# List scheduler of a hybrid SSD and gated-DeltaNet layer: later assumed landings for scratch transfers in DRAM

## The chip, the cores and the metric

The kernel runs on one core of one Trainium2 chip. The metric is the time of one execution in microseconds of device time; the median of several executions is compared. One execution was taken by the hardware profiler, and every row below is from that one.

## The reference

The reference computes one layer of a diffusion backbone in float32: 512 latent tokens and 256 context tokens of width 1024. A conditioning vector gives shifts, scales and gates (adaLN); a projection `w_in` feeds two groups of heads, which run over the tokens forwards and backwards; then come an output projection, an MLP with squared ReLU and a last RMSNorm.

```python
p_lat = modulate(rmsnorm(x, norm1_g[l]), sh1, sc1) @ w_in[l]
p_ctx = modulate(rmsnorm(ctx, norm1_g[l]), sh1c, sc1c) @ w_in[l]
y_lat, y_ctx = token_mixers(p_lat, p_ctx, ...)   # conv, SiLU, SSD scan, gated delta rule
x = x + g1 * (y_lat @ w_out[l])
x = x + g2 * sq_relu_mlp(modulate(rmsnorm(x, norm2_g[l]), sh2, sc2), w_mlp1[l], w_mlp2[l])
...
return rmsnorm(x, final_g)
```

The gated delta rule (`gdn_scan`) needs, for each chunk, the solution of a triangular system with a unit diagonal. The kernel inverts these triangular matrices ahead of the scan.

## The kernel before, in words

Every large product is taken in three parts, since a float32 weight is split into a high part `wH` (ScalarE casts it) and a low part `wL` (GpSimd subtracts); so a projection is 8 blocks of the width times 3 matmuls. `pl_k3` is the accumulator of the fourth key projection over 512 latent tokens (24 matmuls of 128x512), `pc_k3` that over 256 context tokens (24 matmuls of 128x256). The letters are k, q, v, g (heads of the delta rule), x, z, B, C (SSD). The raw weight columns come into two buffers `st_...` that are used in turn: the load of `st_x3` must wait until `st_x2` has been split.

Work in order: the modulation and `h` (0 to 40 us of the span); the projections k, q, g, v, B, C; beside them four inversions b = 0 to 3 (`inverse`, two heads each); then the SSD (`ssd`, eight steps ct = 0 to 7) and four scans (`scan`, 24 dependent steps in all) with the projections x and z as filler; then the output projection in two halves (`wo0a`, `wo1a`), and the MLP (`m1p`, `m2a`).

An inversion (line 671 on, `inverse`) goes through DRAM three times, since blocks change partitions there:

- `At` goes out to `blkD` in four transfers of 32x12x32 elements (rows of 128 bytes) and comes back as `ND`, `YD`. VectorE eliminates inside 32x32 blocks (30 dependent steps, tiles `YD`, `TD`).
- `YD` and `ND` go to `invD`; six loads fill `X`, four `Yf`, four `Yb`, each 48 KB in rows of 128 bytes.
- TensorE joins the blocks in steps that depend on each other, with 32x32 and 64x64 matmuls: `z1` (from `X`), `x1` and `y1` (from `Yf`, `Yb`), `z2`, `y2`; ScalarE copies between them. `Yf` and `Yb` go to `invF`, from where a scan loads them as `Ys`.

The trace leaves numbers out: `z<-X,At` there is z1 and z2 of all inversions.

The order of instructions on each engine is not that of the code. `kernel` traces the program once, and `_plan` builds a graph of it (`_Graph`) and plays it through in a model of the five engines (`_Graph.run`): on each engine the instruction that is ready and has the smallest key goes next. The key is mainly the place in the traced program, less the length of the longest path to the end (`rank`). The order found is then forced on each engine (`_keep`). SP, the engine that issues nearly all DMAs, is one of the five, so DMAs are in an order too: one that waits holds up those behind it. In hardware nothing of the model's times remains, only the order.

What the model assumes of a transfer stands in `_cost` (the time in the shared queue, `gap`, and what passes after it until the landing, `d`) and in `run` (2000 ns more):

```python
gap = b / (380.0 if same else 400.0 if run >= 2048 else 320.0 if run >= 512 else 60.0 if src.startswith("in_") else 150.0)
total = b / (300.0 if src.startswith("in_") else 140.0) + 600.0
d = max(0.0, total - gap)
...
end, fr = queue + self.dur[k] + 2000.0, t + (370.0 if e == 4 else 150.0)
```

`run` in `_cost` is the length of a row in bytes, and a source whose name begins with `in_` is an input of the kernel; every other source counts as scratch: loads from DRAM scratch, stores to it, and the stores of the output. An instruction on TensorE that needs a transfer's data is not ready before `end`; until then the model puts other ready work there.

Of the kernel before, what the change touches and what calls it, by code (L numbers as in the profile page):

```python
# [1394 lines left out]
_WINDOW = 3413.4  # L1395
_SLACK = (0.0, 100.0, 100.0, 100.0, 0.0)
_LANES = 8
_MIX = 1.2e9
_STRETCH = 1.0


def _name(ap):
    return getattr(ap, "memref", None) or ""
# [9 lines left out]
class _Graph:  # L1413
    def __init__(self, nc, tc, traced, ordered):
# [22 lines left out]
        for k, i in enumerate(self.ins):  # L1437
            d, s = set(), set()
# [39 lines left out]
        for i in self.ins:  # L1478
            e = _ENG.index(str(i.engine).split(".")[1])
            self.eng.append(e)  # L1480
            self.dma.append(kind[i.name] == "InstDMACopy")
            self._cost(i, e, kind[i.name], psum)
        for m in range(n):
            deps[m].discard(m)
            self.need[m] = len(deps[m])
            for d in deps[m]:
                same = self.eng[d] == self.eng[m] and not (self.dma[d] and d in sync[m])
                self.succ[d].append((m, same, d in sync[m]))

    def _cost(self, i, e, kind, psum):  # L1490
        table, accum, lock, shape = 0, False, False, 0
        w = _width(i.outs[0])
        gap = None
        if kind == "InstDMACopy":
            src = _name(i.ins[0])
            b = 4
            for q in i.outs[0].ap:
                b *= q[1]
            run = 4 * min(i.ins[0].ap[-1][1], i.outs[0].ap[-1][1])
            same = any(q[0] == 0 and q[1] > 1 for q in i.ins[0].ap)  # L1500
            gap = b / (380.0 if same else 400.0 if run >= 2048 else 320.0 if run >= 512 else 60.0 if src.startswith("in_") else 150.0)
            total = b / (300.0 if src.startswith("in_") else 140.0) + 600.0
            d = max(0.0, total - gap)
        elif e == 0:
            shape = tuple(i.tile_size)
            full = str(i.ins[0].dtype).endswith("float32") and str(i.ins[1].dtype).endswith("float32")
            if i.is_transpose:
                gap = max(84.0, 20 + 0.7 * w)
            elif not full:
                gap = 15 + 0.415 * w  # L1510
            elif shape == (32, 32):
                gap = 34.0
            elif shape[1] < 128:
                gap = 5 + 1.7 * w
            else:
                gap = max(218.0, 5 + 1.7 * w)
            d = gap + 163.0
            shape = (shape, tuple(i.tile_position or ()), full and not i.is_transpose)
        else:
            sp = [a for a in i.ins if hasattr(a, "memref") and _width(a) > 1]  # L1520
            ps = any(_name(a) in psum for a in sp)
            two = len(sp) > 1
            if e == 1:
                lock = not ps and kind != "InstMemset"
                if kind == "InstTensorTensor":
                    d = 145 + 1.04 * w
                elif kind == "InstReciprocal":
                    d = 150 + 6.2 * w
                elif kind == "InstTensorCopy":
                    d = 150 + (1.04 if ps or w >= 1024 else 0.55) * w  # L1530
                elif kind == "InstMemset":
                    d = 130 + 0.5 * w
                else:
                    d = 205 + 1.04 * w if two or ps else 140 + 0.6 * w
            elif e == 2:
                table = _TABLE.get(str(i.func).split(".")[-1], 0)
                accum = len(i.outs) > 1
                one = sum(hasattr(a, "memref") for a in i.ins) == 1
                d = (190 if one else 250) + 0.82 * w + (20 if ps else 0)
            else:  # L1540
                lock = True
                d = 250 + 2.0 * w if kind == "InstTensorTensor" else (130 if kind != "InstMemset" else 90) + 0.95 * w
        self.dur.append(d if e == 0 or gap is not None else d * _STRETCH)
        self.gap.append(gap)
        self.table.append(table)
        self.accum.append(accum)
        self.lock.append(lock)
        self.shape.append(shape)

    def run(self, key):  # L1550
# [3 lines left out]
        soon, now = [[] for _ in range(5)], [[] for _ in range(5)]  # L1554
# [8 lines left out]
        queue, table, shape, holder, held, waiting, done, last = 0.0, 0, None, -1, 0.0, None, 0, 0.0  # L1563
        landed = []

        def finish(k, e, end, fr):
            free[e] = fr
            heapq.heappush(events, (fr, 0, e))
            for m, same, sy in succ[k]:
                q = eng[m]  # L1570
                if same:
                    t = fr
                    if not self.dma[k] and e:
                        if self.dma[m]:
                            t = end + 28
                        elif sy:
                            t = end + (122 if self.accum[k] else 34)
                else:
                    t = end + (50 if self.dma[k] else _LAT[e][q]) + _SLACK[q]
                if t > ready[m]:  # L1580
                    ready[m] = t
                need[m] -= 1
                if need[m] == 0:
                    heapq.heappush(soon[q], (ready[m], key[m], m))
                    if not stalled[q]:
                        heapq.heappush(events, (max(ready[m], free[q]), 0, q))

        while done < n:
            t, what, e = heapq.heappop(events)
            if what:  # L1590
                if waiting is not None and t >= held - 1e-6:
                    k, w = waiting
# [8 lines left out]
            while soon[e] and soon[e][0][0] <= t + 1e-9:  # L1601
                _, p, k = heapq.heappop(soon[e])
                heapq.heappush(now[e], (p, k))
            if not now[e]:
                if soon[e]:
                    heapq.heappush(events, (soon[e][0][0], 0, e))
                continue
            p, k = heapq.heappop(now[e])
            if self.dma[k] and len(landed) >= _LANES and landed[-_LANES] > t:
                heapq.heappush(soon[e], (landed[-_LANES] + 30.0, p, k))  # L1610
                heapq.heappush(events, (t, 0, e))
                continue
# [6 lines left out]
            elif e == 0:  # L1619
                d = self.gap[k]  # L1620
# [4 lines left out]
                shape = self.shape[k]  # L1625
# [59 lines left out]
def _plan(trace):  # L1685

    import concourse.bacc as _bacc
    import concourse.tile as _tile

    nc = _bacc.Bacc("TRN2", target_bir_lowering=False, num_devices=1)  # L1690
    tc = _tile.TileContext(nc)
    tc.__enter__()
    trace(nc, tc)
    traced = list(nc.cur_bb.bb.instructions)
    tc.close()
    tc.compile()
    (ordered,) = tc.compile_state.ordered_instructions_by_block.values()
    graph = _Graph(nc, tc, traced, ordered)
    rank = graph.rank()
    key = [_MIX * k / graph.n - rank[k] for k in range(graph.n)]  # L1700
    _, order = graph.run(key)
    return [[graph.ins[k].name for k in line] for line in order]

# [41 lines left out]
```

## Time and profile before

| | us |
|---|---|
| median of 3 runs (lowest, highest) | 1163.1 (1160.6, 1168.05) |
| the profiled execution | 1160.29 |
| its span, first to last instruction | 1158.6 |
| TensorE matmul busy in the span | 1091.5 |
| mean granted TensorE clock, share of full speed | 0.978 |

The profiled execution is 2.8 us below the median of the runs, and 1.7 us of it lie outside the span. Waits and stretches below are counted from the span's start.

### The profile page before, as it was taken

To read this page: it belongs to the slowest core of one execution; us is meant where nothing else is said; L and a number is where in the kernel's file an instruction comes from. 1 tells how busy PE (TensorE), PEld (TensorE's weight loads), DVE (VectorE), ACT (ScalarE), POOL (GpSimd) and SP (SyncE) were. 2 spreads that over 40 slices of the span, in tenths; PEclk is the share of its full clock that TensorE was granted. 3 is DMA by queue.
4 is the path that set the end of the run, shared out by engine and by line. 5 is a ranking of instruction groups with operands and counts; after the bars stand their busy time and mean duration, and the time that the engine had idled before them with its cause. 6 is when DMAs were issued, how large, how long until landed. Compare 5 with 4: busy or idle time off the path is not lost.

```text
span 1158.6 us, 19228 instructions
## 1 busy us (share of the span) xinstructions
PE 1091.5 (94%) x7120; PEld 885.4 (76%) x7120; DVE 721.4 (62%) x1402; ACT 604.0 (52%) x1419; POOL 456.0 (39%) x386
## 2 busy tenths in 40 slices
PE   5799998998989999999999989999999999999997
PEld 2458877787868777788878868777777888888885
DVE  3775699897979557578766777878673022444023
ACT  4647656648364577578886674125333122444133
POOL 1216444442331332222322254433545445555462
PEclk9899999999999999999999989998999999999999
DMA  9577746686564694745372277743443333333332
GB/s 313 182 198 200 229 146 185 195 227 170 157 163 146 154 347 104 267 123 207 103 273 73 92 282 237 227 136 100 137 146 109 92 107 93 91 103 98 91 104 96
DMA packets 189334, 188.44 MB, mean 163 GB/s; under 512 B 41548, under 2 KB 140153, under 8 KB 189241
## 3 DMA queue, kind: packets, MB, share of 16 engines
q1 hardware_dynamic: 188336, 186.04, 52.6%
q8 instruction: 56, 0.92, 0.3%
q10 hardware_dynamic: 905, 1.18, 0.3%
q14 instruction: 37, 0.30, 0.1%
HBM read 151.45 MB, written 35.73 MB: 162 GB/s over the span
## 4 chain that ended last, share of the span: by engine, by line
PE 70%; DVE 11%; ACT 8%; DMA 6%; issue 3%; SPq 1%; POOL 0%; ACTq 0%; DVEq 0%; POOLq 0%
PE m1p L62 15%; PE m2a L62 15%; PE wo0a L62 4%; PE wo1a L62 3%; PE pl_x L62 3%; PE pl_v L62 3%; PE pl_g L62 2%; PE yp L62 2%; PE op L62 2%; PE pc_v L62 2%; DMA st_q<-in_w_in_dram 2%; PE pp L62 2%; PE pl_z L62 2%; PE up L62 2%; PE pc_x L62 2%
## 5 line engine op out<-in xcount | busy, mean ns | idle before, releaser
L77 POOL TENSOR_TENSOR wL_m<-st_m,wH_m 128x512 fp32r<-128x512 f32 x128 | 177.4, 1405 | 186.6 <-ACT wH_m L68 177.1
L68 ACT ACTIVATE wH_m<-st_m 128x512 fp32r<-128x512 f32 x128 | 77.1, 625 | 187.0 <-PE m2a L62 111.0
L62 PE MATMUL m1p<-h2hL,wH_m 128*128 128x512 f32 (+1 forms) x272 | 104.5, 384 | 1.6 <-DVE h2hL L77 1.5
L62 PE MATMUL m1p<-h2hH,wH_m 128*128 128x512 f32 (+1 forms) x272 | 103.6, 383 | 2.5 <-ACT rl L68 2.0
L62 PE MATMUL m1p<-h2hH,wL_m 128*128 128x512 f32 (+1 forms) x272 | 103.1, 380 | 0.0
L62 PE MATMUL m2a<-wL_m,aH 128*128 128x512 f32 x256 | 99.4, 389 | 0.0
L62 PE MATMUL m2a<-wH_m,aL 128*128 128x512 f32 x256 | 99.4, 389 | 0.0
L62 PE MATMUL m2a<-wH_m,aH 128*128 128x512 f32 x256 | 98.9, 389 | 0.0
L77 DVE TENSOR_TENSOR rtmp<-m2a,g2r 128x512 f32<-128x512 f32 x16 | 10.7, 683 | 140.1 <-PE m2a L62 140.0
L77 DVE TENSOR_TENSOR rl<-rl 128x512 f32<-128x512 f32 x32 | 47.5, 1484 | 51.8 <-ACT rl L68 51.5
L62 PEld LDWEIGHTS m1p<-h2hH,wH_m 128*128 128x128 f32 x272 | 51.8, 191 | 14.0 <-ACT rl L68 4.0
L77 POOL TENSOR_TENSOR wL_wo<-st_wo,wH_wo 128x512 fp32r<-128x512 f32 x32 | 45.2, 1433 | 41.1 <-ACT wH_wo L68 35.4
L74 DVE SCALAR_TENSOR_TENSOR macc<-mw,sil,macc 128x256 f32<-128x256 f32 x84 | 56.4, 671 | 7.2 <-DMA mw<-in_w_mod_dram 5.4
L62 PEld LDWEIGHTS m1p<-h2hL,wH_m 128*128 128x128 f32 x272 | 52.1, 191 | 11.5 <-DVE h2hL L77 2.4
L77 DVE TENSOR_TENSOR TD<-YD,ND 112x30 f32<-112x30 f32 (+14 forms) x120 | 59.6, 497 | 0.9
L62 PEld LDWEIGHTS m1p<-h2hH,wL_m 128*128 128x128 f32 x272 | 52.2, 192 | 9.4
L62 PEld LDWEIGHTS m2a<-wH_m,aH 128*128 128x128 f32 x256 | 48.0, 188 | 10.1
L62 PEld LDWEIGHTS m2a<-wL_m,aH 128*128 128x128 f32 x256 | 48.0, 188 | 10.0
L62 PEld LDWEIGHTS m2a<-wH_m,aL 128*128 128x128 f32 x256 | 48.0, 188 | 9.9
L77 DVE TENSOR_TENSOR YD<-YD,TD 112x30 f32<-112x30 f32 (+14 forms) x120 | 54.5, 454 | 0.9
L665 POOL TENSOR_SCALAR_AFFINE_SELECT rw<-rw 128x512 f32<-128x512 f32 x32 | 24.0, 764 | 64.7 <-ACT er L68 60.6
L68 ACT ACTIVATE wH_wo<-st_wo 128x512 fp32r<-128x512 f32 x32 | 18.5, 623 | 50.0 <-PE wo0a L62 21.6
(496 smaller groups left out, 3224.2 us busy)
## 6 DMA issues: line engine op xcount, KB each, us to landing
st_m<-in_w_mlp_dram SPq DMA_DIRECT2D x64, 512.0 KB
wm<-in_w_mod_dram SPq DMA_DIRECT2D x16, 512.0 KB
rw<-rowsD SPq DMA_DIRECT2D x16, 512.0 KB
st_wo<-in_w_out_dram SPq DMA_DIRECT2D x16, 512.0 KB
mw<-in_w_mod_dram SPq DMA_DIRECT2D x16, 512.0 KB
Ys<-invF SPq DMA_DIRECT2D x8, 768.0 KB
st_k<-in_w_in_dram SPq DMA_DIRECT2D x8, 512.0 KB
st_g<-in_w_in_dram SPq DMA_DIRECT2D x8, 512.0 KB
```

Of the source, the lines that this page charges most:

```text
L62: PE.matmul(o, lhsT=lhsT, rhs=rhs, start=start, stop=stop)
L68: ACT.activation(out=o, in_=i, func=f, **kw)
L74: (eng or DVE).scalar_tensor_tensor(out=o, in0=a, scalar=s, in1=b, op0=op0, op1=op1)
L77: (eng or DVE).tensor_tensor(out=o, in0=a, in1=b, op=op)
L665: POOL.affine_select(out=rw[:, d_], in_=rw[:, d_], pattern=[[0, n], [pat, P]], compare_op=ALU.is_ge, fill=NEG, base=0, channel_multiplier=cm_)
```

## The change

Transfers whose source is no input of the kernel are assumed to land later: by 2500 ns when their rows are shorter than 512 bytes (`_SHORT`), by 800 ns otherwise (`_FROM`). Rows shorter than 512 bytes have the stores of `At` to `blkD`, the loads of `X`, `Yf` and `Yb`, and the two loads of `mod`: 74 transfers. As `rank` takes the same duration, whatever leads up to a scratch transfer also gets a longer path and a slightly smaller key. The model's landing of an `X` load moves from 2.95 to 5.45 us after its turn in the queue. No instruction, tile or transfer is added or taken away.

```diff
+_SHORT = 2500.0
+_FROM = 800.0
+_EARLY = 0.0
+_LATE = 0
+_NEAR = 0.0
...
-            d = max(0.0, total - gap)
+            d = max(0.0, total - gap) + (0.0 if src.startswith("in_") else _SHORT if run < 512 else _FROM)
...
+                    if q == 0 and m < self.scans:
+                        t += _EARLY
...
+            if e == 0 and shape and self.shape[k][0] != shape[0] and _NEAR:
...
+    rows = [k for k in range(graph.n) if graph.dma[k] and _name(graph.ins[k].ins[0]) == "in_w_mod_dram"]
+    for k in rows[24:40]:
+        key[k] += _LATE * _MIX / graph.n
```

`_EARLY`, `_LATE` and `_NEAR` are zero, so the last three pieces change no order.

TensorE at the join of inversion 3, before (`z1_3` are its first matmuls, `pc_x0` the 24 matmuls of the first x projection over the context, of which five have gone ahead of the first two `z1_3`):

```order
L62 MATMUL pc_x0_4528<-hH_120,wH_x0_4476 128x256
L62 MATMUL pc_x0_4528<-hL_121,wH_x0_4476 128x256
L62 MATMUL z1_3_4159<-X_478,At3_3044 32x32 x2
L62 MATMUL pc_x0_4528<-hH_120,wL_x0_4477 128x256
L62 MATMUL pc_x0_4528<-hH_120,wH_x0_4476 128x256
L62 MATMUL pc_x0_4528<-hL_121,wH_x0_4476 128x256
L62 MATMUL pc_x0_4528<-hH_120,wL_x0_4477 128x256
L62 MATMUL pc_x0_4528<-hH_120,wH_x0_4476 128x256
L62 MATMUL z1_3_4159<-X_478,At3_3044 32x32
```

And now (`pl_x1` is the second x projection, over the latent tokens):

```order
L62 MATMUL pc_x0_4528<-hH_120,wL_x0_4477 128x256
L62 MATMUL pl_x1_4824<-hH_120,wH_x1_4519 128x512
L62 MATMUL pl_x1_4824<-hL_121,wH_x1_4519 128x512
L62 MATMUL pl_x1_4824<-hH_120,wL_x1_4520 128x512
L62 MATMUL pl_x1_4824<-hH_120,wH_x1_4519 128x512
L62 MATMUL pl_x1_4824<-hL_121,wH_x1_4519 128x512
L62 MATMUL pl_x1_4824<-hH_120,wL_x1_4520 128x512
L62 MATMUL z1_3_4159<-X_478,At3_3044 32x32 x2
L62 MATMUL pl_x1_4824<-hH_120,wH_x1_4519 128x512
```

All 24 of `pc_x0` and six of `pl_x1` now stand ahead of the first `z1_3`: 19 matmuls of 128x256 and 6 of 128x512 more than before. At inversion 1, 20 of `pc_v1`, 3 of `pl_v2` and 4 transposes more stand there; at inversion 0, 13 of `pl_q6`; at inversion 2, 24 of `pl_v5` and 2 transposes.

SP after inversion 3, before (`rw` are rows for the SSD, `Ys0`, `vtr0`, `kTs0` the loads of the first scan):

```order
L90 DMA rw0_4612<-rowsD_93 128x2x512
L90 DMA rw1_4634<-rowsD_93 128x2x512
L90 DMA invF_106<-Yf_476 128x1536
L90 DMA invF_106<-Yb_477 128x1536
L90 DMA Ys0_0_4647<-invF_106 128x1536
L90 DMA Ys0_1_4648<-invF_106 128x1536
L90 DMA vtr0_4653<-kvD_103 128x768
```

And now:

```order
L90 DMA rw0_4612<-rowsD_93 128x2x512
L90 DMA rw1_4634<-rowsD_93 128x2x512
L90 DMA st_x2_4822<-in_w_in_dram 128x8x128
L90 DMA st_z1_5133<-in_w_in_dram 128x8x128
L90 DMA invF_106<-Yf_476 128x1536
L90 DMA invF_106<-Yb_477 128x1536
L90 DMA st_x3_5376<-in_w_in_dram 128x8x128
L90 DMA Ys0_0_4647<-invF_106 128x1536
L90 DMA Ys0_1_4648<-invF_106 128x1536
L90 DMA vtr0_4653<-kvD_103 128x768
```

The loads `st_x2` and `st_z1` stood ahead of all these before and now stand just ahead of the stores to `invF`; `st_x3` stood 17 places below the first `Ys0`, behind all loads of the first scan, and now stands ahead of them; it waits for GpSimd to free its buffer. `Ys0` waits for no engine.

TensorE at the end of the last scan, before (`yt6` are the first transposes of its result, `pl_x7` and `pc_x7` the last x projection, `yp6` the output of SSD step 6):

```order
L62 MATMUL pl_x7_7781<-hH_120,wL_x7_7640 128x512
L65 MATMUL yt6_7619<-ident_75,oT3_7004 128x128
L62 MATMUL pl_x7_7781<-hH_120,wH_x7_7639 128x512
L65 MATMUL yt6_7619<-ident_75,oT3_7004 128x128 x2
L62 MATMUL pl_x7_7781<-hL_121,wH_x7_7639 128x512
```

And now:

```order
L62 MATMUL pc_x7_7782<-hH_120,wL_x7_7640 128x256
L65 MATMUL yt6_7619<-ident_75,oT3_7004 128x128
L62 MATMUL pc_x7_7782<-hH_120,wH_x7_7639 128x256
L65 MATMUL yt6_7619<-ident_75,oT3_7004 128x128
L62 MATMUL pc_x7_7782<-hL_121,wH_x7_7639 128x256
```

Ahead of the first `yt6` there now stand 9 matmuls of `pl_x7`, 12 of `pc_x7` and 16 of `yp6` more, so that these no longer lie between the last scan and the output projection.

## Rows read from the trace of the kernel before

**Rows 1.** The page's head and its first part: span, and TensorE's busy time.
```profile
span 1158.6 us, 19228 instructions
PE 1091.5 (94%) x7120; PEld 885.4 (76%) x7120; DVE 721.4 (62%) x1402; ACT 604.0 (52%) x1419; POOL 456.0 (39%) x386
```

**Rows 2.** Busy time by stretch: us, busy (instructions) per engine, PEclk, DMA share, GB/s.
```profile
264.00:288.00 24.00, 20.53 (x400) 16.87 (x399) 18.95 (x48) 20.44 (x57) 7.10 (x7) 0.93 0.61 151
412.00:440.00 28.00, 26.32 (x180) 21.75 (x179) 21.32 (x35) 17.18 (x42) 10.38 (x9) 1.00 0.84 308
440.00:660.00 220.00, 214.60 (x1517) 179.07 (x1517) 155.66 (x407) 167.83 (x509) 59.38 (x53) 1.00 0.48 157
660.00:700.00 40.00, 35.23 (x215) 28.82 (x212) 27.26 (x38) 26.04 (x52) 19.16 (x15) 0.91 0.68 235
880.00:1158.60 278.60, 270.79 (x1195) 223.86 (x1193) 76.23 (x82) 85.56 (x158) 139.74 (x102) 0.99 0.32 97
```

**Rows 3.** TensorE's waits over the span: us in total, times, longest us.
```profile
PE y L62 <- issue: 7.0, 4, 3.8
...
PE z L62 <- DMA X<-invD: 4.4, 2, 2.4
...
PE yp L62 <- issue: 2.9, 2, 2.3
...
PE pc_k L62 <- DVE cy_k L74: 2.6, 1, 2.6
...
PE wo0a L62 <- ACT yhH L68: 2.4, 1, 2.4
...
PE pl_x L62 <- ACT wH_x L68: 1.4, 1, 1.4
```

**Rows 4.** The chain of work around inversions 1 and 3: start us, us, what.
```profile
266.89 5.47 DMA X<-invD
...
392.34 3.51 DMA X<-invD
...
436.57 0.22 PE pp L62 x2
```

**Rows 5.** Busy time by stretch, as in rows 2, around the waits of inversions.
```profile
268.00:274.00 6.00, 3.40 (x19) 2.29 (x18) 5.86 (x19) 5.94 (x14) 3.83 (x4) 0.97 0.80 114
274.00:280.00 6.00, 6.00 (x158) 5.60 (x159) 5.90 (x14) 4.16 (x13) 0.00 (x0) 0.74 0.93 262
344.00:352.00 8.00, 8.00 (x114) 6.30 (x114) 5.18 (x14) 4.91 (x11) 0.00 (x0) 0.70 0.23 86
392.00:400.00 8.00, 5.99 (x34) 5.26 (x33) 2.96 (x4) 0.78 (x1) 0.00 (x0) 0.79 0.67 134
```

**Rows 6.** DMA queues from 339 to 344 us: packets, MB, share of 16 engines.
```profile
q8 instruction: 1, 0.02, 1.3%
```

**Rows 7.** Timeline of SP and POOL between 411 and 427 us: start us, us, instruction.
```profile
412.45 0.33 SPq L90 DMA_DIRECT2D invF<-Yb  x1
412.83 1.37 SPq L90 DMA_DIRECT2D Ys<-invF  x2
421.70 0.32 SPq L90 DMA_DIRECT2D vtr<-kvD  x1
...
424.83 1.36 POOL L77 TENSOR_TENSOR wL_x<-st_x,wH_x 128x512 fp32r<-128x512 f32 x1 [0.34 <-ACT wH_x L68]
```

**Rows 8.** The chain from the last scan to the output projection: start us, us, what.
```profile
655.86 0.11 PE yt L65
...
659.46 1.68 PE yp L62 x28
...
661.80 2.86 PE pc_x L62 x24
664.66 5.48 PE pl_z L62 x24
...
678.51 0.96 ACT yhH L68
```

More of the change, by code (lines that the diff above doesn't have):

```diff
@@ L1482, in __init__ @@
             self._cost(i, e, kind[i.name], psum)
+        self.scans = min(k for k, i in enumerate(self.ins) if _name(i.outs[0]).startswith("Ys"))
         for m in range(n):
@@ L1608, in run @@
             p, k = heapq.heappop(now[e])
+            if e == 0 and shape and self.shape[k][0] != shape[0] and _NEAR:
+                for q, m in heapq.nsmallest(12, now[0]):
+                    if self.shape[m][0] == shape[0] and q < p + _NEAR:
+                        now[0].remove((q, m))
+                        now[0].append((p, k))
+                        heapq.heapify(now[0])
+                        p, k = q, m
+                        break
             if self.dma[k] and len(landed) >= _LANES and landed[-_LANES] > t:
```

## Prediction

> **What bounds the kernel now.** I read four views. The page's head comes first: TensorE is busy for 1091.5 of 1158.6 us [rows 1], so no change of order can win more than the 67 us in which it is idle and what a low clock costs it. The stretches say where that is. From 880 us on the MLP keeps TensorE full, and the order there hardly changes; during the scans it is busy for 214.60 of 220 us; the gaps lie in the joins of the inversions, 20.53 of 24 us around the second, and where the scans hand over to the output projection, 35.23 of 40 [rows 2]. The waits name them: 7.0 us in four waits at `y`, for nothing that the profile shows; 4.4 us in two waits of `z` for the `X` loads; 2.4 us of `wo0a` for ScalarE; 1.4 us of an x projection for its weights' cast [rows 3]. The chain shows those `X` loads as its links, 5.47 us from one issue to the matmul in inversion 1 and 3.51 in inversion 3 [rows 4], where the model of before assumed 2.95. That is the place the change aims at. The reader should also see what follows such a wait: the granted clock is 0.97 in the 6 us that hold the wait of inversion 1 and 0.74 in the 6 us behind it; around the wait of inversion 3 it is 0.79 over 8 us [rows 5]. These are parts at 1.2 GHz among parts at 2.4 GHz, each behind a wait of TensorE of 2 us or more.
>
> **The change part by part.** Work is only moved, so I price places.
>
> Waits for `X`. The two cost 4.4 us [rows 3]. A matmul of 128x512 takes its place every 5.48/24 = 0.228 us, one of 128x256 every 2.86/24 = 0.12 [rows 8]. In inversion 3, 19 x 0.12 + 6 x 0.228 = 3.6 us more work now stand ahead of the first `z1`, against a wait of 4.4 - 2.4 = 2.0; in inversion 1, 20 x 0.12 + 3 x 0.228 = 3.1 us and four transposes, against 2.4. So both waits are covered, unless the loads come later by as much. -4.4 us. Inversions 0 and 2 are put back too, by 13 x 0.228 = 3.0 and 24 x 0.228 = 5.5 us, and had no such wait: nothing is won there.
>
> The clock behind them. If the waits go, so does the low stretch behind each: 6 x (1 - 0.74) = 1.6 us and 8 x (1 - 0.79) = 1.7 us [rows 5]. -3.2 us. Bounds: 0, if shorter waits remain that lower the clock as well, and -3.2.
>
> The load `st_x3`. Its weights' cast held TensorE for 1.4 us [rows 3]. On SP the load now stands ahead of `Ys0`, so the cast can come earlier. -1.4 us.
>
> What that load holds up. It needs the buffer of `st_x2`, free when GpSimd's second `wL_x2` ends, 424.83 + 1.36 = 426.2 us in this trace, 13.7 us after the second store to `invF` at about 412.5; `Ys0` was issued at 412.83 [rows 7]. All loads of the first scan now stand behind this wait. The cover so far: the scan's first matmul, `pp`, came only at 436.57 [rows 4], and the loads behind `Ys` not before 421.70 [rows 7]. New: the join of inversion 3 ends 9 x 0.228 + 10 x 0.12 = 3.2 us of work later (9 of `pl_x1` and 10 of `pc_x1` more stand ahead of its last `y2`) and 7.6 us of waits and low clock earlier, so 4.4 earlier; if the split follows it as before, `Ys0` is issued at 426.2 - 4.4 = 421.8. Ahead of `pp` must then land two `Ys` of 768 KB and four loads of 384 KB, 3.1 MB, at the 308 GB/s of this stretch [rows 2] 10.2 us: 432.0. TensorE, with the same work ahead of `pp` to within 0.2 us, gets there at 436.57 - 7.6 = 429.0 and waits 3.0. Bounds: 0, if the split comes 3 us sooner (the SSD rows that ScalarE works on in between are now loaded ahead of `st_x2`), and +7.4, if it ends at 426.2 again. I take +3.0, which keeps the distance that the rows show.
>
> The end of the scans. The scans keep the order of their 24 steps, and x and z projections fill between. Now 9 x 0.228 + 12 x 0.12 + 16 x 0.06 = 4.4 us more of that filler (`yp`: 1.68/28) stand ahead of the last scan's end, and so 4.4 us less behind it [rows 8]. From `yt` at 655.86 to the cast `yhH` at 678.51 there are 22.7 us [rows 8] of stores, loads and casts that the filler covered but for the 2.4 us of `wo0a` [rows 3]. What is won ahead of the scans is therefore partly given back here. Bounds: 0, if the `yp7` matmuls, which now stand ahead of `wo0a`, need as long, and +4.4, if all of the missing filler shows as wait. I take +2.4, the wait that this place has today.
>
> The rest of the order (convolutions on VectorE, copies on ScalarE) is shuffled in many small ways that the trace can't price. The nearest row is the longest wait of TensorE on VectorE, 2.6 us [rows 3]: two such waits can go, two can come. I take 0 and keep -5.2 and +5.2 for the range.
>
> Sum: -4.4 - 3.2 - 1.4 + 3.0 + 2.4 = -3.6 us, from 1160.3 for the profiled execution to 1156.7. That execution lies 2.8 us below the median of the runs, so the forecast for the median is 1159.5.
>
> Two rules of the Trainium skill bear on this. The trace has `X` loads of 48 KB that took 5.47 and 3.51 us from issue to use [rows 4]. The Trainium skill, "DMA: Bandwidth & Descriptors", section "Anatomy of one DMA — SWDGE (gpsimd) path", gives a fixed 2.0 us plus the bytes at 436 GB/s, by which I estimate 2.1 us for such a load, and says the fixed part doesn't grow. By that rule the landing assumed before was late enough, and the change would only put back the four joins; the trace disagrees by 1.4 to 3.4 us, with the DMA engines at a share of 0.80 around the first of the two [rows 5]. The other is at `y`, and the sum differs by it: see the second rival.
>
> **The rivals.** First, all is given back. The scans' chain, not TensorE, would then set the end: what the inversions win is waited for at `pp` and behind the last scan. For it speaks that `wo0a` already waits, that the filler behind the scans shrinks by 4.4 us, and that `pp` hangs on a split; against it, that `pp` had its data to spare before. With the upper bounds at both places, -9.0 + 7.4 + 4.4 = +2.8; with the lower at the end, -1.6: the time stays at 1163.1, within 3 us.
>
> Second, the four waits at `y` are landings too. `y` reads `Yf` and `Yb`, whose loads the change also lets land 2.5 us later, so that the 7.0 us [rows 3] could go with the others, and the low clock of 0.70 over 8 us behind the longest [rows 5], 2.4 us. Time: 1159.5 - 7.0 - 2.4 = 1150.1. Against it speaks that the profile names no transfer for these waits, and that in the 5 us around the longest one packet of the instruction queue went through, 0.02 MB [rows 6]: they come in the run of small matmuls, where TensorE gets through its instructions fastest. The Trainium skill, "Runtime: NRT & Kernel Launch", section "Terms", says that an engine's instruction memory is refilled in blocks of 16 KiB, and the packet has that size; by that rule these waits are for code, and stay.
>
> Third, slower: the scan starts late. If the split of `st_x2` ends at 426.2 as it did and the 3.1 MB then move at the 235 GB/s of the other crowded stretch, 660 to 700 us [rows 2], they take 13.2 us and `pp` comes at 439.4, 2.8 us after today; the whole chain of 24 steps follows. TensorE has then waited at `pp` for the better part of 10 us, and a low stretch behind that costs 1.7, as behind the wait of inversion 3. Sum: +2.8 + 1.7 - 1.4 for the cast + 2.4 at the end = +5.5, and 1168.6. It turns slower than today from the point where the split ends after 426.2 - 5.5 = 420.7, at that rate, and slower by over 1% where it ends after 432.
>
> **How the numbers follow.** The forecast (1 to 8 us won) has 0.42, all given back 0.25, the waits at `y` going too 0.13, the late scan 0.20. One per cent is 11.6 us, about what a measurement of this kernel can tell from no change. Below 1151.5 lie the second rival and a small part of the forecast, where the shuffle wins its 5.2 us as well and nothing is lost at `pp` (1151.3): 0.15 in all. Above 1174.7 lies the late scan if a shuffle of 5.2 us comes on top or the split ends later still, half of its chance: 0.10. The range goes from 1149.5, just beyond the second rival, to 1171, beyond the late scan by half a shuffle.
>
> **What would show it right or wrong.** In the trace of the changed kernel the waits of `z` for `X` should be under 1 us together and the clock near 1.0 in the 8 us behind the first `z` of inversions 1 and 3. The waits at `y` should still be there, 4 to 9 us without a named transfer. SP should issue `Ys0` at 419 to 424 us, behind `st_x3`; at 426 or later the third rival holds. `pp` should start at 430 to 434 after a wait of about 3 us for `Ys` or `vtr`. Behind the last `yt`, waits of `wo0a` and `yp` of 5 to 8 us in all, where they are 2.4 + 2.3 = 4.7 today [rows 3], would confirm what is given back; 10 us there would mean the first rival. The forecast is wrong if the MLP starts later than today, whatever the waits of `z`.

## The result and the profile after

| | before | after |
|---|---|---|
| median (lowest to highest, executions) | 1162.39 us (1156.77 to 1169.58, 20) | 1170.30 us (1166.88 to 1174.14, 20) |
| ratio to before, 95% interval | 1 | 1.0063 [1.0046, 1.0079] |
| the profiled execution | 1160.29 us | 1171.28 us |

The changed kernel is 7.3 us slower by the ratio (5.3 to 9.2). That is less than the one per cent that the prediction took for what a measurement can tell, but 20 executions tell it from no change, and it lies on the other side of the forecast, which was 3.6 us faster. The profiled pair lies further apart than the medians, by 11.0 us. In it TensorE's busy time grew by 4.0 us [rows 1] and its idle time by 7.0. The lower clock takes 3.7 us more (2.5% of 1169.6 us against 2.2% of 1158.6), but the busy time also changed for other reasons, as the `yp` below show.

The page's head and its first part, after:

```profile
span 1169.6 us, 19221 instructions
PE 1095.5 (94%) x7120; PEld 889.3 (76%) x7120; DVE 723.8 (62%) x1402; ACT 606.1 (52%) x1419; POOL 455.4 (39%) x386
```

TensorE's waits after: us in total, times, longest us.

```profile
PE h2p L65 <- ACT h2f L68: 8.9, 1, 8.9
PE y L62 <- issue: 7.7, 4, 2.5
PE yp L62 <- ACT HG L68: 4.8, 1, 4.8
...
PE st L62 <- issue: 3.9, 1, 3.9
...
PE yp L62 <- issue: 1.1, 1, 1.1
```

Beside [rows 3]: the 4.4 us of `z` for `X`, the 1.4 of `pl_x` for its cast and the 2.4 of `wo0a` are gone. New are 8.9 us at `h2p` (the transposes ahead of the MLP), 4.8 at `yp` and 3.9 at `st`. The waits at `y` stayed.

Busy time by stretch after, with the columns of [rows 2]:

```profile
264.00:288.00 24.00, 20.86 (x392) 17.25 (x393) 17.28 (x39) 17.84 (x46) 6.54 (x7) 0.86 0.46 117
268.00:274.00 6.00, 6.00 (x125) 4.75 (x124) 5.67 (x15) 6.00 (x21) 0.00 (x0) 1.00 0.56 155
...
392.00:400.00 8.00, 8.00 (x48) 6.23 (x46) 5.85 (x9) 2.72 (x5) 2.52 (x2) 1.00 0.60 121
412.00:422.00 10.00, 6.10 (x35) 5.20 (x32) 3.60 (x12) 7.16 (x20) 1.56 (x3) 0.66 0.75 250
412.00:440.00 28.00, 23.05 (x148) 18.56 (x145) 15.44 (x27) 16.35 (x40) 11.24 (x9) 0.88 0.71 254
440.00:660.00 220.00, 216.84 (x1482) 179.04 (x1480) 153.49 (x401) 162.30 (x485) 57.98 (x53) 1.00 0.49 161
...
790.00:810.00 20.00, 11.06 (x60) 9.52 (x59) 16.57 (x41) 11.72 (x24) 5.47 (x4) 0.74 0.45 119
```

Set against [rows 2, 5]: in the two stretches at the `X` waits TensorE is now full and at a granted clock of 1.00. But over all of 264 to 288 us it is busy as long as before (20.86 against 20.53) at a lower clock (0.86 against 0.93), and between 412 and 440 it is idle for 5 us, where it was busy for 26.32 us at 1.00. So the gap moved within the inversions. The scans keep TensorE a little busier (216.84 against 214.60 of 220 us), and yet take longer. The last row is the new gap: 9 idle us of 20, and much of the rest at the lower of the two clock levels.

Along the program, by named instructions in the timelines of the two: the first `pp` of the scans comes 4.5 us later than before (440.9 against 436.4, which the chain in [rows 4] puts at 436.57), the last `yt` ends 12.9 later (671.2 against 658.3), the first `wo0a` starts 12.7 later (692.2 against 679.5), and the first `m1p` of the MLP 15.4 later (802.1 against 786.7). Of these 15.4 us 11.0 are left at the end. All of the loss of this pair stands ahead of the last `yt`: from there to the end the changed kernel takes 498.4 us, before 500.3. This does not mean that nothing was lost behind it, since some filler had left that part (below). The prediction named the later start of the MLP as what would make it wrong: "The forecast is wrong if the MLP starts later than today, whatever the waits of `z`."

**The handover to the MLP, which the prediction had not read.** The chain of waits after: start us, us, what.

```profile
794.70 4.46 DMA mw<-in_w_mod_dram
...
799.18 0.36 DVE macc L81
...
800.58 0.09 DVE G L74
...
800.69 0.57 ACT h2f L68
...
801.31 1.14 PE h2p L65 x4
```

The timeline of SP says what the links are (start us, us, instruction). Before:

```profile
777.80 0.24 SPq L90 DMA_DIRECT2D gD<-br  x1
778.91 0.39 SPq L90 DMA_DIRECT2D mod<-gD  x1
```

And after, with SP's rows around the join of inversion 3 ahead of it:

```profile
414.18 1.38 SPq L90 DMA_DIRECT2D invF<-Yb  x1
426.50 0.38 SPq L90 DMA_DIRECT2D st_x<-in_w_in_dram  x1
426.94 1.04 SPq L90 DMA_DIRECT2D Ys<-invF  x2
...
788.90 0.22 SPq L90 DMA_DIRECT2D gD<-br  x1
792.77 0.39 SPq L90 DMA_DIRECT2D st_m<-in_w_mlp_dram  x1
793.21 0.57 SPq L90 DMA_DIRECT2D mod<-gD  x1
...
794.70 1.13 SPq L90 DMA_DIRECT2D mw<-in_w_mod_dram  x2
```

`mod` holds the MLP's shift and scale, which the kernel itself has stored to scratch (`gD`). It is loaded in rows of 4 bytes, so it is one of the 74 transfers that got 2.5 us, and its stores got 0.8. For the model this data now lands so late that other work goes first: on SP the load `st_m`, which waits for a buffer until 792.77; on VectorE a `macc` (the next modulation's products), which waits for the load `mw` behind that. The timeline of VectorE, first before, then after:

```profile
781.51 0.16 DVE L74 SCALAR_TENSOR_TENSOR G<-mod,vcol 128x8 f32<-128x8 f32 x1
```

```profile
799.18 0.35 DVE L81 TENSOR_SCALAR macc<-mw,sil 128x256 f32<-128x256 f32 x1 [1.67 <-DMA mw<-in_w_mod_dram]
...
800.49 0.16 DVE L74 SCALAR_TENSOR_TENSOR G<-mod,vcol 128x8 f32<-128x8 f32 x1
```

`G`, from which ScalarE makes `h2f`, the input of the MLP, comes at 800.49 instead of 781.51. Two queues hold it up, one after the other.

### The profile page after: what moved, and what is told of

Read it like the earlier page. It is cut to its first block, busy times and chain, and to the rows that moved or that the text cites. A ratio compares the mean times of both kernels' runs of the same rounds, so it can differ in the third digit from the quotient of the medians.

```text
span 1169.6 us, 19221 instructions
## 1 busy us (share of the span) xinstructions
PE 1095.5 (94%) x7120; PEld 889.3 (76%) x7120; DVE 723.8 (62%) x1402; ACT 606.1 (52%) x1419; POOL 455.4 (39%) x386
## 4 chain that ended last, share of the span: by engine, by line
PE 75%; DVE 11%; ACT 6%; DMA 4%; issue 3%; SPq 0%; POOL 0%; ACTq 0%; POOLq 0%; DVEq 0%
PE m1p L62 15%; PE m2a L62 15%; PE wo0a L62 4%; PE wo1a L62 4%; PE pl_x L62 3%; PE pl_z L62 3%; PE yp L62 2%; PE op L62 2%; PE pl_g L62 2%; PE pp L62 2%; PE pl_q L62 2%; PE up L62 2%; PE pl_k L62 2%; DVE YD L77 2%; PE pc_x L62 2%
## 5 line engine op out<-in xcount | busy, mean ns | idle before, releaser
L74 DVE SCALAR_TENSOR_TENSOR macc<-mw,sil,macc 128x256 f32<-128x256 f32 x84 | 59.5, 708 | 6.9 <-DMA mw<-in_w_mod_dram 5.2
L77 DVE TENSOR_TENSOR YD<-YD,TD 112x30 f32<-112x30 f32 (+14 forms) x120 | 60.3, 502 | 0.8
L77 DVE TENSOR_TENSOR TD<-YD,ND 112x30 f32<-112x30 f32 (+14 forms) x120 | 56.6, 471 | 2.9 <-issue 1.9
L77 POOL TENSOR_TENSOR wL_z<-st_z,wH_z 128x512 fp32r<-128x512 f32 x16 | 22.2, 1406 | 57.2 <-ACT wH_z L68 42.8
```

The source lines that it names most:

```text
L74: (eng or DVE).scalar_tensor_tensor(out=o, in0=a, scalar=s, in1=b, op0=op0, op1=op1)
L77: (eng or DVE).tensor_tensor(out=o, in0=a, in1=b, op=op)
```

## The experiments

Three theories stood at the start. **H**: the handover costs the loss. **S**: the scans cost it, through a late start or a worse mix of matmuls (theory C below is a sharper form of it). **I**: the inversions' new order itself costs it. Each ratio is to the kernel before, measured beside it. Edits stand shortened: `move(engine, what, ahead_of)` moves instructions in the finished list of one engine, just before the list is forced; `mod2`, `G2`, `macc5` are the second modulation load, the `G` and the `macc` of the handover, `wo1a2` the third tile of `wo1a`. No run leaves out or changes a part of the computation.

**The load of `mod` ahead of `st_m` on SP.**

```diff
     _, order = graph.run(key)
+    move(SP, mod2_second_load, ahead_of=st_m1_2)
```

> Theory H (handover): TensorE waits 8.9 us at h2p because G2, the MLP's modulation, is late for two reasons at once: on SP its load mod2 stands behind st_m1_2, which waits for GpSimd, and on VectorE G2 stands behind three macc5 that need mw5 loads issued after mod2. This kernel is the changed one with only the SP place undone: mod2 goes ahead of st_m1_2. H: mod2 is issued at 789 to 791 instead of 793.2, but G2 still comes at 798 to 801 behind macc5, the wait at h2p stays 7.5 to 9 us and the time within 2 us of the changed kernel (1168 to 1172). Rival Q (the SP queue alone delays it): the wait falls by about 4 us, 1166. Rival S (the late scan, Ys0 behind st_x3 on SP, is what costs): no change at all.

Ratio 1.0052 [1.0031, 1.0073]. The timelines of SP and of VectorE in this run:

```profile
791.94 0.39 SPq L90 DMA_DIRECT2D mod<-gD  x1
```

```profile
800.96 0.16 DVE L74 SCALAR_TENSOR_TENSOR G<-mod,vcol 128x8 f32<-128x8 f32 x1
```

The load goes out earlier, but `G` does not move, and `h2p` still waits 7.5 us: VectorE's queue holds it too.

**The same, and `G` ahead on VectorE.**

```diff
+    move(SP, mod2_second_load, ahead_of=st_m1_2)
+    move(DVE, G2, ahead_of=wo1a2)
+    move(DVE, four_macc5, ahead_of=next_macc5)
```

> The changed kernel with both places undone: mod2 ahead of st_m1_2 on SP, and on VectorE G2 ahead of the work on the third tile of wo1a, the first four macc5 behind the first four pairs of casts. H: G2 at 791 to 793, the wait at h2p falls from 8.9 us to 0 to 2, one or two low-clock stretches of 1.7 us behind it go too; up to 4 us of it may come back in the MLP, which in the kernel before lost that much there. Time 4 to 10 us under the changed kernel: 1160 to 1166. Rival S: under 2 us won. Rival L (the rows of the modulation themselves are late, since their last store to gD is issued at 788.9 instead of 777.8): the wait stays at 3 to 5 us and 3 to 5 us are won, 1165 to 1167.

Ratio 1.0101 [1.0060, 1.0142]: a miss. `G` came at 792.17 as meant, yet the timeline of ScalarE shows `h2f` behind the norm of other tiles:

```profile
796.42 1.06 ACT L68 ACTIVATE xn<-x 128x1024 f32<-128x1024 f32 x1 [0.21 <-DVE x L77]
...
797.81 1.00 ACT L68 ACTIVATE h2f<-h2p,mod,G 128x256 f32<-128x256 f32 x2
```

`h2p` waits 10.1 us in two pieces. There is a third queue, and moving pieces by hand in two of them made it worse.

**No surcharge for `gD`.** Here the model decides all queues itself.

```diff
-  (0.0 if src.startswith("in_") else _SHORT if run < 512 else _FROM)
+  (0.0 if src.startswith("in_") or "gD" in (source, target) else _SHORT if run < 512 else _FROM)
```

> The change without its surcharge for the stores to gD and the loads from it (mod2 among them); all other scratch transfers keep theirs. The order is that of the changed kernel up to the output projection, and there the scheduler itself puts mod2 ahead of st_m1_2 and G2 ahead of macc5. H: as the kernel with both places undone by hand, wait at h2p 0 to 2 us, 1160 to 1166. S: as the changed kernel, 1169 to 1171. L: 1165 to 1167.

1167.12 us, 1.0047 [1.0024, 1.0070]; the wait at `h2p` halves. In time and wait this is nearest to rival L, not to H. TensorE's waits:

```profile
PE h2p L65 <- ACT h2f L68: 4.6, 1, 4.6
```

**`st_x3` behind the loads of the first scan again** (the prediction's term of +3.0, and its third rival).

```diff
+    move(SP, st_x3, ahead_of=first_yD0)
```

> The changed kernel with st_x3 put back behind the ten loads of the first scan on SP. H: Ys0 is issued at 414 to 418 instead of 426.9, but the first pp stays at 439 to 442, since in the changed kernel it came without a wait; the time within 2 us of the changed kernel, 1168 to 1172. S: pp comes at 436 to 438 and the time falls by 3 to 7 us, 1163 to 1167.

1.0066 [1.0043, 1.0088]: nothing is won. The timelines of SP and TensorE in this run:

```profile
420.40 0.88 SPq L90 DMA_DIRECT2D invF<-Yb  x1
421.33 2.30 SPq L90 DMA_DIRECT2D Ys<-invF  x2
```

```profile
445.67 0.28 PE L62 MATMUL pc_x<-hH,wH_x 128*128 128x256 f32 x1
445.79 0.39 PE L62 MATMUL pp<-vtr,Ys 128*128 128x128 f32 x2
```

`Ys` now goes out right behind the stores, and `pp` still comes when the filler ahead of it is through: it starts straight behind a `pc_x`, 0.12 us after its start. (It comes later than in the changed kernel because this execution ran at 0.95 over its first 229 us, against 0.98.) In the changed kernel `Ys` was issued at 426.94, as late as the prediction's upper bound (426.2), and `pp` did not wait either; the timeline of its TensorE, here and in the scans, with `x2`, `x4` for a run of alike matmuls:

```profile
411.60 1.09 PE L62 MATMUL st<-xw,Bt 128*64 128x128 f32 x14
416.59 0.69 PE L62 MATMUL st<-xw,Bt 128*64 128x128 f32 x4 [3.90 <-issue]
...
440.79 0.28 PE L62 MATMUL pc_x<-hH,wH_x 128*128 128x256 f32 x1
440.91 0.39 PE L62 MATMUL pp<-vtr,Ys 128*128 128x128 f32 x2
...
512.74 0.43 PE L62 MATMUL yp<-rw,xt 128*64 128x128 f32 x2
513.10 0.71 PE L62 MATMUL pp<-r,Ys 128*128 128x128 f32 x4
513.75 0.43 PE L62 MATMUL yp<-rw,xt 128*64 128x128 f32 x2
```

**The two orders spliced.** The planner is played twice, with and without the surcharges; the order of one is kept up to a model time (`cut`), the other's behind it.

```diff
+    head, tail = play(2500.0, 800.0), play(0.0, 0.0)
+    cut = model_time(first "pp0")
+    order = [a_before(cut) + rest_of(b) for a, b in zip(head, tail)]
```

New up to the first `pp`, old behind it (theory I):

> The scheduler is played twice, with and without the change; each engine takes the changed order for all that the model issues before the first pp of the first scan, and the order of before for the rest. Theory C: between the end of the scans (last yt) and the MLP's first matmul lie 128 to 131 us that no order of TensorE shortens (the modulation rows of the MLP on VectorE, 8 dependent rounds), so the time follows the end of the scans; the changed order is bad because it ends the scans later, by filler and by its start. C for this kernel: the waits of z for X stay gone, the scans take 222 us as before, the last yt ends at 651 to 656, and the time is 1154 to 1160, under the kernel before. Rival H (handover): what was lost lies behind the scans alone; also under before, 1154 to 1160. Rival I (the inversions give back what they win before pp starts, by fetches of code and a low clock): 1161 to 1165, no better than before.

1166.46 us, 1.0038 [1.0014, 1.0062]: not below before, as C and H wanted, but above, and nearest to I. The waits of `z` for `X` are gone, but `pp` comes at 441.4 us, 5.0 later than before, and the last `yt` ends at 666.0 instead of 651 to 656. The new inversions win nothing even with the old scans and handover behind them.

Old up to the first `pp`, new behind it:

> The other half: the order of before up to the first pp, the changed order from there on. C: the scans take 228 to 231 us instead of 222, the last yt ends at 666 to 672, and the MLP starts 128 to 131 us behind it: 1170 to 1176, as slow as the changed kernel or slower by the waits for X. H: much of it at the handover, 1168 to 1174 too, but with the scans as long as before. I: 1163 to 1168.

1168.14 us, 1.0045 [1.0022, 1.0069]. By the ratios both halves cost, each somewhat more than half of the whole. The scans take 229.2 us, as C expected, but the time lies under C's range and at the meeting of H's and I's, so this run alone decides for none of them.

New up to the first `yt6` (the end of the scans), then old:

> The changed order up to the first yt of the last scan, the order of before from there on: the handover alone is undone, all of it, while the scans end as late as in the changed kernel. C: last yt at 669 to 673, MLP 128 us behind it instead of 131, time 1166 to 1169. H: the wait at h2p is gone and the time is that of before or better, 1159 to 1164.

1167.43 us, 1.0037 [1.0016, 1.0058], and no wait at `h2p` but 0.2 us. That is 2.9 us less than the changed kernel by the medians, for its 8.9 us of wait and the clock behind it, and the intervals of the two ratios overlap. C's time came true and H's did not. C's premise fell, though: the MLP starts 123.4 us behind the last `yt`, not 128 to 131, so an order can shorten this part.

**One surcharge at a time.**

```diff
-_FROM = 800.0
+_FROM = 0.0
```

> The surcharge of 2500 ns for short rows alone, none for other scratch transfers. In its order st_x3 stands behind the loads of the first scan, mod2 ahead of st_m1_2 and G2 ahead of macc5, as before; ahead of the last yt stand 2.6 us of matmuls more than before, ahead of z1_1 2.0 us fewer and ahead of z1_3 4.8 us more. C: of the waits for X that of inversion 3 goes (2.0 us and 1.7 of low clock), that of inversion 1 stays or grows by up to 2; the scans' end moves by +2.6 - 3.7 + 0 to 2, so 1161 to 1164, the same as before. H: without the handover's swap nothing is lost, 1158 to 1162. If short rows are what costs: 1168 to 1171.

1157.22 us, 0.9971 [0.9943, 0.9999], under all the ranges expected, by little under H's.

```diff
-_SHORT = 2500.0
+_SHORT = 0.0
```

> The surcharge of 800 ns for the other scratch transfers alone, none for short rows. st_x3 stands ahead of Ys0 as in the changed kernel, mod2 and G2 stand as before; 11.8 us of matmuls more than before lie ahead of the last yt, yp is cut into 48 runs in the scans (45 before, 53 with the change). If the 800 ns carry the loss: 1165 to 1170. If the loss needs both surcharges (the handover's swap comes only with both): 1160 to 1164.

1174.92 us, 1.0119 [1.0087, 1.0151], over both ranges expected. So the loss belongs to the small surcharge. The 2500 ns for short rows, to which the prediction gave nearly all its room, are a gain of 3.4 us by the ratio (0.1 to 6.6). `st_x3` stands ahead of `Ys` only with the 800 ns; `mod` falls behind in both queues only with the two together.

**The output matmuls of the SSD kept together.** The changed order cuts the `yp` matmuls among the scans into 53 runs (before: 45). In this edit the last twelve of the sixteen of each SSD step stand together, 27 runs in all.

```diff
+    for c in range(8):
+        yp = [k for k in order[PE] if name(k).startswith("yp%d_" % c)]
+        put yp[4:16] together, where the last of them stands
```

> Theory Y: in the scans the changed order cuts the yp matmuls (tile 128x64) into 53 runs between scan matmuls (tile 128x128) instead of 45; two yp between others take 0.36 us of TensorE, two in a block of 30 take 0.13, so each run more costs at least 0.23 us though it counts as busy. This kernel is the changed one with the last 12 of the 16 yp of each SSD step (in the program; 24 of 32 in the trace) moved together to the place of the last: 27 runs instead of 53. Y: 26 x 0.23 = 6 us and more of TensorE's time ahead of the last yt go, and the scans take 238 to 246 us from the first pp to wo0a instead of 251: 1160 to 1166. Rival D (the scans go by their chain of dependent steps): nothing, or later yp costs, 1168 to 1173.

1166.46 us, 1.0038 [1.0018, 1.0058]: 3.8 us less than the changed kernel by the medians, 2.9 by the ratios, whose intervals overlap. From `pp` to the last `yt` it takes 226.2 us instead of 230.3, and 247.2 to `wo0a`, where Y wanted 238 to 246. Its TensorE (timeline), to be held against the rows from 512.74 on above:

```profile
512.39 0.39 PE L62 MATMUL yp<-er,HG 128*64 128x128 f32 x4
512.61 0.39 PE L62 MATMUL yp<-rw,xt 128*64 128x128 f32 x4
```

Four `yp` (128x64 weights) take a place every 0.22 us here, 0.11 a pair; between `pp` (128x128 weights) one pair took 0.36 us, 512.74 to 513.10. By stretch, from the first `pp` to the first `wo0a`, the `yp` alone (us, busy of PE, weight loads, VectorE, PEclk, DMA, GB/s), before:

```profile
436.30:679.50 243.20, 23.92 (x192) 13.02 (x192) 4.48 (x6) 1.00 0.50 166
```

after:

```profile
440.80:692.20 251.40, 27.52 (x196) 14.53 (x196) 4.47 (x6) 0.99 0.50 166
```

and with the matmuls together:

```profile
438.30:685.60 247.30, 18.65 (x196) 12.11 (x196) 4.47 (x6) 0.99 0.50 170
```

**The same in the short-row kernel and in the kernel before.**

> The surcharge for short rows alone with the yp of each step together as in the kernel just described: 24 runs instead of 43. Y: 19 x 0.23 = 4.4 us under the kernel with short rows alone, 1151 to 1155. D: 1156 to 1160.

1154.94 us, 0.9941 [0.9919, 0.9964]: faster than the changed kernel and than before, 6.9 us below before by the ratio. Under the short-row kernel it lies by 2.3 us, half of what Y wanted, and the intervals of these two overlap. Its profiled execution has a span of 1152.0 us at a granted clock of 0.984.

> The kernel before with the yp of each step together: 20 runs instead of 45. Y: 25 x 0.23 = 5.8 us under it, 1155 to 1159. D: 1161 to 1166.

1162.39 us, 1.0001 [0.9982, 1.0021]: Y misses, D holds. The busy time of `yp` fell here too, but TensorE's idle time from `pp` to the last `yt` rose from 5.4 to 10.2 us, 4.0 of it at `pp` for ScalarE's `pv` (before: 0.3). That fits D: with the old order the scans go by the chain of 24 steps. It is read from these waits and not tried by itself.

**All together.** The changed kernel without the surcharge for `gD`, and its `yp` together:

> The changed kernel with two parts undone: no surcharge for stores to gD and loads from it (so mod2 and G2 stand as before), and the last 12 of the 16 yp of each SSD step together. Theory P (three parts: inversions about 4, yp about 4, handover about 3 us): 1170 - 4 - 3 = 1162 to 1165. Rival M (something else in the new order of the scans): 1166 to 1169, since the two parts then only shift the wait from one place to the next.

1164.12 us, 1.0001 [0.9982, 1.0019]. With the two edits the whole loss is gone, as P expected. It is not undone stretch by stretch: the last `yt` still ends at 668.3 us, 10.0 later than before, and the time is made up behind it (493.3 us to the end against 500.3).

The same, with the old inversions up to the first `pp`:

> All three parts undone: the order of before up to the first pp, from there the changed order without the surcharge for gD and with the yp of each step together; st_x3 stands ahead of Ys0. P: 1159 to 1163, the time of the kernel before. M: 1165 to 1168.

1163.54 us, 0.9996 [0.9977, 1.0014], the same as the run before it, and half a microsecond over P's range. Here the new order of the inversions is worth nothing, in either direction; but with the old one the last `y2` ends at 411.1 us instead of 414.6, and `pp` still comes at 440.3 instead of 441.1, since more matmuls (178 against 155) stand between the two. So the seam takes back most of what the old inversions won.

## Why the prediction was wrong

**The waits for `X` (-4.4) and the clock behind them (-3.2).** The waits went: there is no row of `z` for `X`. The low clock went behind inversion 3 (1.00 in 392 to 400). Behind inversion 1 it only moved: in 274 to 280 us, where the prediction read 0.74, it is 0.87, and in the 8 us after that 0.67. The first of these stretches, after:

```profile
274.00:280.00 6.00, 4.03 (x157) 3.08 (x151) 5.83 (x11) 2.90 (x6) 2.77 (x2) 0.87 0.73 211
```

The step that failed is that the time stays won. From the end of inversion 0 (228.9 us before, 228.3 after) to `pp` the granted clock is 0.97 before and 0.94 after, so 11.9 us are lost to it there against 6.8, where the sum has 3.2 less. The last `y2` of inversion 3 ends at 411.7 us, where it ended at 411.4 and where the prediction's working gives 411.4 + 3.2 - 7.6 = 407.0; TensorE came to other waits in the same joins. These wait for no transfer of data: 7.7 us at `y` and, new, 3.9 at `st` (416.59 above), with the clock at 0.66 from 412 to 422, mostly the level of 1.2 GHz. If TensorE's records (matmuls, weight loads and its few others) are numbered from 0, the long ones between 278 and 417 us come at record 3777, 5057, 6337 and 6593. These lie multiples of 256 apart. In the traces of all the other runs, before's among them, the waits of over 1.4 us without a releaser at `y`, `z`, `st` and `v0t` fall on the same numbers or, in inversion 0, on 2497 and 2753, which fit the same steps; which of them is long enough to see differs. With the short-row surcharge alone, record 3777 is a `v0t`, and it is `v0t` that waits (its TensorE, timeline):

```profile
280.67 0.60 PE L65 MATMUL v0t<-ident,vT 128*128 128x128 f32 x4 [2.40 <-issue]
```

In the 5 us around the wait at `st` one packet of an instruction queue of the size of [rows 6] goes by (DMA queues, 412 to 417 us: packets, MB, share of 16 engines):

```profile
q8 instruction: 1, 0.02, 1.2%
```

The times of these packets in the traces bear it out. The one for the wait at `st` lands at 415.18 us, and TensorE goes on at 416.59; in all the traces each of these waits ends 1.2 to 1.7 us behind the landing of such a packet (16384 bytes). So TensorE waits for code there, as the prediction read it at `y`. (The Trainium skill, "Runtime: NRT & Kernel Launch", section "Terms", has the refill in blocks of 16 KiB; the trace agrees, with one packet of 0.02 MB for this wait.) The waits at `yp` without a releaser (2.3 us before, up to 5.0 with the new inversions ahead of the old order) stand at other numbers, 4.7 us or more behind the last such packet; what they are for stays open. What the prediction missed, by these traces, is that a wait for data can hide one for code: TensorE that isn't held up at `z` gets to the next boundary sooner and waits there. In the kernel before inversion 3 has its wait for `X` and none at record 6337; without the first the second appears. That the one causes the other is read from these orders and not tried by itself, and a short wait does not hide all: with the 800 ns alone, inversion 3 has 0.9 us for `X` and 2.1 at record 6337.

**`st_x3`: +3.0 at `pp`, -1.4 for the cast.** The cast's wait went. The move on SP came as described, later even than forecast: `Ys` was issued at 426.94 us, by the prediction's own sign a case for its third rival. Its price was 0: `pp` came 14.0 us behind the issue of `Ys`, held up by filler alone, and putting the load back won nothing (1.0066). The step that failed is "436.57 - 7.6 = 429.0" for TensorE's arrival at `pp`: with the waits for code and the low clock of the section above it got there at 440.9 by itself, long enough for the 10.2 us of transfers from 426.9.

**The end of the scans (+2.4) and the scans themselves (0, with 5.2 to each side).** From the last `yt` to the first `wo0a` the changed kernel takes 21.0 us, before 21.2, though filler has left this stretch. The 2.4 us of `wo0a` for `yhH` gave way to `yp` for `HG` (4.8) and `st` for `xw` (1.4). TensorE is idle there for 6.2 us, before for 2.4, so nearly all of the filler that left shows as wait: the term came out near its upper bound (+4.4), where the prediction took +2.4. The stretch has no fixed length: with the old order behind the same scans (the splice at `yt6`) it takes 16.3 us, with 2.4 us of wait as before. Busy time by stretch, with the columns of [rows 2], before, after and in that splice:

```profile
658.29:679.51 21.22, 18.78 (x119) 15.22 (x117) 15.00 (x20) 15.78 (x34) 9.81 (x9) 1.00 0.79 274
671.20:692.23 21.03, 14.86 (x84) 11.48 (x82) 16.74 (x27) 16.95 (x38) 14.95 (x12) 0.90 0.74 263
671.46:687.73 16.27, 13.87 (x70) 11.03 (x69) 13.35 (x18) 14.27 (x30) 9.80 (x9) 1.00 0.84 308
```

Ahead of it, from `pp` to the last `yt`, the changed kernel takes 230.3 us against 221.9, 8.4 more. TensorE is nearly full there, so the filler that moved in lengthens it: 6 `pl_x`, 23 `pc_x` and 28 `yp` more and 20 `st` fewer in the trace, about 4.3 us by the rates in the prediction and 1.09/14 = 0.08 for an `st`. That the prediction's 4.4 is so near is luck. It multiplies 16 `yp` of the program by a rate for one `yp` of the trace, where each is two (its sum should be 5.4), and it leaves out the `st`. Much of the other 4.1 us is `yp`: 27.52 - 23.92 = 3.6 for nearly the same matmuls, made slower by what stands beside them (an upper figure, since the spans of neighbours overlap a little). The step that failed there is pricing matmuls by kind from a block of their own (`yp` at 1.68/28 = 0.06 us), and so taking for free an order that mixes kinds. With it falls the bound that no order can win more than TensorE's idle time and the clock, since its busy time follows the order too. The edit that keeps the `yp` together gave back 3.8 us by the medians. It is not simply an undoing, since it leaves fewer runs than there were before, and in the old order it won nothing.

**"From 880 us on ... the order there hardly changes".** From 880 on TensorE's busy share is the same as before (97%), but nothing was read between 700 and 880. The front part counted `mod` among the 74 transfers; the prediction gave it no step. This is the term that was left out: 8.9 us of wait at `h2p`, with the clock at 0.74 from 790 to 810. In this pair 4.4 us come back in the MLP, from the first `m1p` to the end; no run tries why. Of its cost the old handover gives back 2.9 us, the planner without the `gD` surcharge 3.2, both by the medians.

**The rivals.** The first (all given back) came nearest in outcome for the inversions: with the rest mended they are worth nothing (1163.54 against 1164.12 us, within intervals of 2 us to each side). Its mechanism is half right: `pp` waited for nothing, but behind the last scan its upper bound came. The second (waits at `y` are landings) falls: they stay, at fixed records, whatever instruction stands there. The third gave 1168.6 us, near the 1170.3 measured, but by a mechanism that has no cost; the number was right by accident. The 2.1 us that the prediction estimates from the Trainium skill for an `X` load are for DMAs that GpSimd issues, and SP issues these; neither the sum nor a chance used them.

**The size.** Undone one at a time, the handover gives back about 3 us, the `yp` 3.8, the inversions' order 2.2 (1168.14 against 1170.3). The intervals of the two ratios compared overlap each time, so none of these is shown by itself. The first two together give back 6.2 by the medians, and the ratio is 1.0001 [0.9982, 1.0019] against 1.0063 [1.0046, 1.0079]: this is shown. That these two are the loss, and not two gains that happen to cover it, is argued from the stretches. They overlap, so the loss can't be split into exact shares. Two things stay open: why the 800 ns alone cost more (1.0119) than with the 2500 ns, since its profiled execution was far faster than its median (1167.41 against 1174.92); and why the new inversions cost 4.4 us ahead of the old order (1.0038), if they cost nothing ahead of the mended new one. The seam of the splice, where the work between the last `y2` and `pp` changes, may be a part of it.

With 2500 ns alone the sum forecast (-3.6) came out (-3.4), by luck: that kernel does not have the move of `st_x3`, for which the sum has +3.0 and -1.4. Two waits at `y` are gone there, and the `X` waits with them.

## What to carry to other kernels

A number in a scheduler's model moves every instruction that depends on it, not only the one it was fitted on: list all transfers of the class, and read the trace at each of them, above all where the kernel stores something and loads it back. Price an order by neighbours, not by kind: one pair of matmuls with another weight shape than its neighbours' cost three times what a pair costs in a block, and all the `yp` of the scans 1.5 times (27.52 against 18.65). And a wait that is removed is won only if the next one on the same engine isn't a wait for code.

## What the runs showed of the hardware

TensorE's waits for code stand multiples of 256 of its records apart, end 1.2 to 1.7 us behind the landing of a 16384-byte packet, and last up to 4.4 us (at `st`, in the splice at `yt6`). They show where many small matmuls stand ahead of them; an order changes which instruction meets them and how long they are, not where they stand in the count.

A pair of `yp` between matmuls with 128x128 weights took 0.36 us, in a block 0.11.

The clock differs between executions of one order. From (1 - granted clock) times the span, TensorE lost 25.4 us a run in the mean before, 28.6 after, 21.5 in the fastest version; single runs of the changed kernel lie between 22.1 and 32.8. So some 3 of the 8 us between the medians are clock, and one profile can't tell a microsecond or two of it.
